# Layer 1's K, Q and V scaled by bounds, wider weight blocks, two maps apart, first weights on another queue

## The chip, the cores and the metric

One core of one Trainium2 chip. The metric is the device time of one execution of the kernel in microseconds (us). The inputs lie in device memory (HBM) in f32 before the execution starts, and the output is written there.

## The reference

A backbone of two layers over 1024 latent and 256 context tokens of width 1024. The normalisation comes after the branch, the modulation `h = x * (1 + scale) + shift` ahead of it. Layer 0 is multi-head latent attention with 16 heads, layer 1 differential attention with 8 heads: each head has two attention maps over the same values.

```python
def combine(o1, o2, gate):
    o = o1 - lam_full.astype(o1.dtype) * o2
    o = rms_norm(o, g_sub) * (1.0 - lambda_init)
    return gated(o, gate)
q, k, v, gate = jnp.split(t @ w_in, 4, axis=-1)
...
s = jnp.einsum('bqhgd,bkhd->bhgqk', qb, k).astype(jnp.float32) * scale
p = jax.nn.softmax(s, axis=-1).astype(v.dtype)
return jnp.einsum('bhgqk,bkhv->bqhgv', p, v)
...
x = layer_norm(DEEPNORM_ALPHA * x + gate[:, None, :] * (o @ out_w[i]), ln_g[i], ln_b[i])
```

In layer 1 q, k and v have 64, 64 and 128 columns per map and head; q and k of the latent tokens get a rotary embedding; the latent queries see all 1280 keys, and the context's own output isn't needed.

## The kernel before, in words

Layer 0 fills the span up to 825 us, its output projection (`out_tile`) goes to 986 us. That projection leaves h of layer 1 as two fp16 parts, `h1H` and `h1L`: for each tile of 128 tokens VectorE (DVE) multiplies the transposed tile by the modulation's scale (L917, into `hb`), GpSimd (POOL) adds the shift (L919), ScalarE (ACT) casts to fp16 (L922), and POOL takes the rest (L923).

Every product of layer 1 is made of three fp16 matmuls (`mm3`, L185 to L187): high by high, high by low, low by high. To make the two parts, `split16` (L181, L182) scales an f32 tile by a power of two and casts it on ACT, and DVE takes the rest. The scale comes from `pow2_of` (L284 to L287), four tiny DVE instructions.

`prod_w(h, which)` loads the weights of a head: `which` 0 is the 256 columns of Q and K, 1 those of V and the gate. Four DMAs of 256 KB from SyncE's queue (SP) bring `ws`; ACT sums the squares (L977, `wsq`); a matmul with ones (L981) adds them over the partitions; DVE and POOL make the scale of it (L983 to L988, `uw`); `split16` makes `wH` and `wL` of each block.

`prod_k1`, `prod_q1` and `prod_v1` make K, Q and V of a head. The rotary embedding leaves K in `kr`; its largest value is taken on DVE (L1064), and `split16` scales by it (`kH`, `kL`; ACT and DVE). Q takes the reciprocal scale. V is evicted from PSUM to `Vf`, the gate to `gg` (L1125, L1126, ACT), both scaled by the weights' scale; DVE takes V's maximum over the row (L1132), a step later the matmul L1141 turns it round, and `split16`'s two halves make `vh` and `vl`.

`scores1` does one tile of 128 queries for both maps. PE computes a PSUM bank of scores of the 256 context keys for the two maps (the first bank), then two banks of 512 keys for each map (L1166, L1167); DVE takes a maximum, negated, of each (L1179, L1183), the smallest of two (L1184), and of these and the context's (L1186, times the softmax scale); ACT takes the exponential of each bank with it (L1189, into `p`), with the sums. Then DVE combines the two maps into one (L1192 to L1195). `turn1` turns the combined map 128 columns at a time (PE, L1202) and splits it (`ph`, `pl`); `values1` multiplies by V (L1210 to L1212).

The order. In layer 1 PE's instructions stand in the order in which the code issues them; those of the other engines are put in order by a scheduler, with a higher priority for scores, turns and values. All engines take their queue in order. `step1` issues one step: scores of tile t, values of tile t-2, then the three turns (4, 4 and 2 blocks) of tile t-1, and after each of the four a slot of side work (`some`), which spends a credit of 3600 matmul columns (`SLOT1`) on a generator that makes the next head's K and Q, then V, with the weights of the sets that follow woven in at the steps of `WAT`. A head has eight steps. A step's maxima of K and V (`later`) are issued at its end. Tiles of PSUM come from eight banks in turn.

Before the first head runs (986 to 1050 us), `prod_w(0, 0)` and `prod_w(0, 1)` are issued in full, then head 0's K, Q and V. During head 6 there is no weight set left, and the output weights of layer 1 (`out_w1`, 512 columns at a time) are loaded in their place; the last head has the output projection beside it, and opens with `out_open`, which converts the other output weights (L1239, L177).

```python
for (k0, n), v in zip(((0, 4), (4, 4), (8, 2)), at[1:]):
    if pc is not None:
        with tc.high_priority(HP):
            turn1(pc, ph, pl, k0, n)
    some(side, v)
```

## Time and profile before

| what | value |
|---|---|
| median of 3 runs | 1907.2 us (1903.72 to 1908.63) |
| the profiled execution | 1901.87 us |
| its span in the trace | 1900.1 us |
| mean granted clock of TensorE | 0.965 of full |
| busy: PE, DVE, ACT, POOL | 1700.0, 1318.6, 1108.2, 853.0 us |

The profile is of one execution. PE is TensorE's matmul stream, PEld its loads of stationary operands, which overlap. A row of a timeline gives an instruction's start, its length, engine, line, operation, output and inputs; in brackets it has how long the engine was idle before it, and what ended that. A row of waits gives who waited for whom: us in total, times, the longest.

### The profile page before, as it was taken

How to read it: one execution, taken by the hardware profiler on the slowest of the kernel's cores; microseconds unless marked ns; L12 is line 12 of the kernel's file. 1: busy time of each engine (PE TensorE's matmuls, PEld its weight loads, DVE VectorE, ACT ScalarE, POOL GpSimd, SP SyncE). 2: the span in 40 equal slices, each digit the busy share in tenths (PEclk: the TensorE clock that was granted, in tenths of full speed). 3: DMA queues.
4: the chain of work that ended last, by engine and by line, in shares of the span. 5: the costliest groups of instructions: out<-in, count | busy, mean ns of one | idle time of the engine just before them, and what ended most of it. 6: DMA issues, size and time to landing. Idle time of an engine off the chain costs nothing. (4 is left out here: it accounts for less than half of the span.)

```text
span 1900.1 us, 37206 instructions
## 1 busy us (share of the span) xinstructions
PE 1700.0 (89%) x14482; PEld 1239.3 (65%) x14482; DVE 1318.6 (69%) x2396; ACT 1108.2 (58%) x2245; POOL 853.0 (45%) x748
## 2 busy tenths in 40 slices
PE   7899979989899899968869999999999999887898
PEld 4888945656566565556656576767676767665776
DVE  7546476595665767626754778787878787987774
ACT  3442157767677678811123677776777676766542
POOL 1441036757667676746652223232232233433544
PEclk9999989999999999979989999999999999999899
DMA  8255531131211212153333111211121212213341
GB/s 297 65 136 151 167 92 40 41 83 24 75 44 32 66 43 76 51 172 132 112 123 98 42 54 47 58 47 48 50 53 42 63 41 64 74 41 132 100 129 67
DMA packets 117663, 155.43 MB, mean 82 GB/s; under 512 B 14591, under 2 KB 85855, under 8 KB 117486
## 3 DMA queue, kind: packets, MB, share of 16 engines
q1 hardware_dynamic: 111726, 147.80, 26.3%
q10 hardware_dynamic: 5760, 5.25, 0.8%
q8 instruction: 114, 1.87, 0.4%
q14 instruction: 63, 0.52, 0.1%
HBM read 99.17 MB, written 27.08 MB: 66 GB/s over the span
## 5 line engine op out<-in xcount | busy, mean ns | idle before, releaser
L709 POOL TENSOR_TENSOR pl<-p,ph 128x1024 f16<-128x1024 f32 (+1 forms) x176 | 367.8, 2095 | 173.6 <-ACT ph L708 154.3
L1189 ACT ACTIVATE p<-ps_b,mx 128x512 f32<-128x512 f32 (+1 forms) x384 | 233.1, 622 | 67.1 <-DVE mx L1186 67.1
L707 ACT ACTIVATE p<-ps_a,esc 128x1024 f32<-128x1024 f32 (+1 forms) x176 | 189.2, 1075 | 123.1 <-PE ps_a L765 116.4
L689 DVE TENSOR_REDUCE mx<-ps_a 128x1 f32<-128x1024 f32 x128 | 155.2, 1221 | 105.1 <-PE ps_a L687 104.9
L708 ACT CAST ph<-p 128x1024 f16<-128x1024 f32 (+1 forms) x176 | 177.2, 1007 | 5.5
L1183 DVE TENSOR_REDUCE mx<-ps_b 128x1 f32<-128x512 f32 x256 | 166.2, 681 | 1.0 <-PE ps_b L1167 0.3
L182 DVE SCALAR_TENSOR_TENSOR pl<-ps_b,lcf,ph 128x512 f16<-128x512 f32 (+1 forms) x192 | 122.7, 655 | 63.4 <-ACT ph L181 63.3
L778 PE MATMUL ps_d<-Vh,pl 128*128 128x65 f16 x1344 | 151.7, 195 | 7.3 <-POOL pl L709 6.0
L775 PE MATMUL ps_d<-Vh,ph 128*128 128x65 f16 x1344 | 154.8, 196 | 0.0
L777 PE MATMUL ps_d<-Vl,ph 128*128 128x64 f16 x1344 | 153.4, 194 | 0.0
L185 PE MATMUL ps_b<-h1H,wH 128*128 128x512 f16 (+1 forms) x384 | 134.0, 349 | 12.5 <-ACT p L1189 12.5
L185 PE MATMUL ps_b<-wH,h1H 128*128 128x256 f16 x512 | 139.5, 272 | 5.6 <-ACT p L1189 5.6
L1166 PE MATMUL ps_b<-KS,QS 128*128 128x512 f16 (+1 forms) x384 | 129.4, 354 | 11.7 <-DVE pl L182 7.7
L775 PEld LDWEIGHTS <-ph 128*128 128x128 f16 x1344 | 125.0, 98 | 22.6 <-issue 5.6
L187 PE MATMUL ps_b<-wH,h1L 128*128 128x256 f16 x512 | 139.5, 273 | 0.0
L186 PE MATMUL ps_b<-wL,h1H 128*128 128x256 f16 x512 | 139.5, 272 | 0.0
L763 PE MATMUL ps_a<-qH,KH 100*128 100x512 f16 x320 | 123.7, 387 | 15.0 <-DVE qH L699 7.5
L181 ACT ACTIVATE ph<-ps_b,lcf 128x512 f16<-128x512 f32 (+1 forms) x192 | 119.4, 636 | 29.8 <-PE ps_b L1202 29.7
L777 PEld LDWEIGHTS <-ph 128*128 128x128 f16 x1344 | 125.6, 99 | 16.1 <-issue 0.6
L186 PE MATMUL ps_b<-h1L,wH 128*128 128x512 f16 (+1 forms) x384 | 134.2, 349 | 0.0
L187 PE MATMUL ps_b<-h1H,wL 128*128 128x512 f16 (+1 forms) x384 | 133.9, 349 | 0.0
L1167 PE MATMUL ps_b<-KS,Q 128*128 128x512 f16 (+1 forms) x384 | 132.4, 353 | 0.0
(380 smaller groups left out, 5202.3 us busy)
## 6 DMA issues: line engine op xcount, KB each, us to landing
adw<-in_ada_w SPq DMA_DIRECT2D x64, 256.0 KB, 2.9
ws<-in_dw SPq DMA_DIRECT2D x64, 256.0 KB, 3.0
g<-sg_d SPq DMA_DIRECT2D x18, 512.0 KB
adaw<-in_ada_w SPq DMA_DIRECT2D x16, 512.0 KB, 5.4
sg_d<-gg ACTq DMA_DIRECT2D x40, 128.0 KB, 2.9
o<-o_d SPq DMA_DIRECT2D x10, 512.0 KB, 9.0
o_d<-op SPq DMA_DIRECT2D x7, 640.0 KB
xt<-in_xT SPq DMA_DIRECT2D x16, 256.0 KB, 2.6
```

The costliest lines, as they stand in the source:

```text
L185: pe.matmul(ps, aH, bH, start=start, stop=False, skip_group_check=skip)
L186: pe.matmul(ps, aH, bL, start=False, stop=False, skip_group_check=skip)
L187: pe.matmul(ps, aL, bH, start=False, stop=stop, skip_group_check=skip)
L689: dve.tensor_reduce(mx[:, t, 0:1], ps, axis=AX.X, op=ALU.max)
L707: act.activation(p32[:, :n], st, AF.Exp, scale=esc0)
L708: act.copy(ph[:, :n], p32[:, :n])
L709: pool.tensor_tensor(pl[:, :n], p32[:, :n], ph[:, :n], op=ALU.subtract)
L775: pe.matmul(pv[:, t, :], ph[:, ts], Vh[:, k, h, :], start=(k == kcs[0] and t == 0), stop=False, skip_group_check=True)
L777: pe.matmul(pv[:, t, :V0], ph[:, ts], Vl[:, k, h, :], start=False, stop=False, skip_group_check=True)
L778: pe.matmul(pv[:, t, :], pl[:, ts], Vh[:, k, h, :], start=False, stop=(k == NT - 1), skip_group_check=True)
L1183: dve.tensor_reduce(mx[:, 2 + 2 * m + i:3 + 2 * m + i], b, axis=AX.X, op=ALU.max, negate=True)
L1189: act.activation(p[m][:, c0:c0 + n], b, AF.Exp, bias=nb, scale=sc1, accum_out=sm[:, 2 + 3 * m + i:3 + 3 * m + i])
```

## The change

- `h1_range`, which runs once before layer 1, makes constant scales: `kc1` for K and V, `hic` and `vic` for the others. The maxima of K (L1064) and of V (L1132), the matmul L1141, and the scales that hung on them are removed. V and the gate are evicted with plain copies; the scale of the gate goes into the Silu. Q is scaled by `es1`, which takes in the softmax scale, so L1184 and L1186 are one instruction, and the exponential has no scale.
- A weight set comes in two DMAs of 512 KB, and its squares and splits are of 1024 columns (half as many); `out_w1` likewise. The tags `ws`, `wL` and `wH` keep their bytes, in half as many buffers (3, 4 and 4 in place of 6, 8 and 8). `WAT` has five places in place of nine.
- `scores1` yields after each map: in `step1`, a side slot stands between the first map's scores and the second's. Five slots of 2900 columns take the place of four of 3600. The last head's order stays.
- `prod_w(0, 0)` is loaded from ACT's queue. `prod_w(0, 1)` is woven into head 0's K and Q instead of being issued ahead of them.

```diff
-WAT = ((6, 10, 14, 18, 23, 28, 32, 36, 39), (3, 7, 11, 15, 20, 25, 29, 33, 36))
+WAT = ((6, 14, 21, 27, 34), (3, 10, 18, 25, 32))
...
-QK1 = 16.0
 PW = 16.0
-SLOT1 = 3600, 3600, 3600, 3600
-SLOTO = 7000, 7000, 7000, 7000
+SLOT1 = 2900, 2900, 2900, 2900, 2900
+SLOTO = 0, 7000, 7000, 7000, 7000
...
         for i in range(2):
             dve.tensor_reduce(hm[:, i:i + 1], ab1[:, i, :, :].rearrange("p a b -> p (a b)"), axis=AX.X, op=ALU.max,
                               apply_absolute_value=True)
-        dve.scalar_tensor_tensor(hm[:, 2:3], hm[:, 0:1], 1.01 * D ** 0.5, hm[:, 1:2], op0=ALU.mult, op1=ALU.add)
-        pe.matmul(bk[:, :P], hm[:, 2:3].to_broadcast([P, P]), idn, start=True, stop=True)
-        dve.tensor_reduce(hm[:, 3:4], bk[:, :P], axis=AX.X, op=ALU.max)
-        dve.tensor_scalar_max(hm[:, 3:4], hm[:, 3:4], 1e-30)
-        pow2_of(hsc, hun, hm[:, 3:4], 16384.0, hm[:, 0:2])
+            pe.matmul(bk[:, i * P:(i + 1) * P], hm[:, i:i + 1].to_broadcast([P, P]), idn, start=True, stop=True)
+        dve.tensor_reduce(hm[:, 2:4], bk[:, :2 * P].rearrange("p (a b) -> p a b", a=2), axis=AX.X, op=ALU.max)
+        R = D ** 0.5
+        dve.tensor_scalar(hm[:, 2:3], hm[:, 2:3], 1.01 * R, 1e-30, op0=ALU.mult, op1=ALU.add)
+        dve.tensor_tensor(hm[:, 4:5], hm[:, 2:3], hm[:, 3:4], op=ALU.add)
+        dve.scalar_tensor_tensor(hm[:, 5:6], hm[:, 3:4], R, hm[:, 2:3], op0=ALU.mult, op1=ALU.add)
+        pow2_of(hsc, hun, hm[:, 4:5], 16384.0, hm[:, 6:8])
+        dve.tensor_tensor(hm[:, 5:6], hm[:, 5:6], hsc, op=ALU.mult)
+        pow2_of(kc1, kci, hm[:, 5:6], 2.0 ** -5, hm[:, 6:8])
+        dve.tensor_scalar_mul(hic, kci, SC1)
...
-    def prod_w(h, which, bank_=lambda: bank("b")):
+    wt, un, us1, es1 = {}, {}, {}, {}
+
+    def prod_w(h, which, bank_=lambda: bank("b"), load=sp):
         wt[which] = []
         ws, sq = [], w1("sq")
-        for q in range(4):
+        for q in range(2):
             ws.append(w1("ws"))
-            sp.dma_start(ws[q], dw[q * 256:(q + 1) * 256, h, which * 256:(which + 1) * 256].rearrange(
+            load.dma_start(ws[q], dw[q * 512:(q + 1) * 512, h, which * 256:(which + 1) * 256].rearrange(
                 "(k p) c -> p k c", p=P))
-            if q % 2:
-                yield 0
-        for q in range(4):
+        yield 0
+        for q in range(2):
             act.activation(w1("wsq"), ws[q].rearrange("p a b -> p (a b)"), AF.Square, accum_out=sq[:, q:q + 1])
-            if q % 2:
-                yield 0
+        yield 0
         bk = bank_()
-        pe.matmul(bk[:, :4], ones, sq, start=True, stop=True)
+        pe.matmul(bk[:, :2], ones, sq, start=True, stop=True)
         u, p2 = w1("uw"), w1("uw")
-        dve.tensor_reduce(u[:, 0:1], bk[:, :4], axis=AX.X, op=ALU.add)
+        dve.tensor_reduce(u[:, 0:1], bk[:, :2], axis=AX.X, op=ALU.add)
         pool.tensor_scalar(u[:, 0:1], u[:, 0:1], 1.01, 1e-30, op0=ALU.mult, op1=ALU.add)
         pool.tensor_tensor(u[:, 0:1], u[:, 0:1], poshalf, op=ALU.pow)
         pow2_of(u[:, 1:2], u[:, 0:1], u[:, 0:1], 16384.0, p2)
-        dve.tensor_scalar(u[:, 0:1], u[:, 0:1], hun, 1.0 if which else QK1 ** 0.5, op0=ALU.mult, op1=ALU.mult)
+        dve.tensor_tensor(u[:, 0:1], u[:, 0:1], hun, op=ALU.mult)
+        if which:
+            us1[h] = w1("us")
+            pool.tensor_tensor(us1[h], u[:, 0:1], vic, op=ALU.mult)
+        else:
+            es1[h] = w1("es")
+            dve.tensor_scalar(es1[h], u[:, 0:1], u[:, 0:1], hic, op0=ALU.mult, op1=ALU.mult)
         un[which] = u[:, 0:1]
         yield 0
-        for q in range(4):
+        for q in range(2):
             wH, wL = w1("wH"), w1("wL")
             split16(wH, wL, ws[q], u[:, 1:2])
-            wt[which] += [(wH[:, j, :], wL[:, j, :]) for j in range(2)]
+            wt[which] += [(wH[:, j, :], wL[:, j, :]) for j in range(4)]
             yield 0
-    for which in range(2):
-        for _ in prod_w(0, which, lambda: bank("c")):
-            pass
+    for _ in prod_w(0, 0, lambda: bank("c"), act):
+        pass
...
+    dve.tensor_tensor(vic, kci, lcf[:, 1:2], op=ALU.mult)
...
         def fin():
-            dve.tensor_reduce(kq[:, 2:3], kr, axis=AX.X, op=ALU.max, apply_absolute_value=True)
-            dve.tensor_scalar_max(kq[:, 2:3], kq[:, 2:3], 1e-30)
-            pow2_of(kq[:, 0:1], kq[:, 1:2], kq[:, 2:3], 256.0, w1("p2s"))
-            dve.tensor_scalar(kq[:, 1:2], kq[:, 1:2], uq, uq, op0=ALU.mult, op1=ALU.mult)
             H, L = w1("kH"), w1("kL")
-            split16(H, L, kr, kq[:, 0:1])
+            split16(H, L, kr, kc1)
...
-            split16(H, L, rr, ksc[h][:, 1:2])
+            split16(H, L, rr, es1[h])
...
-        act.activation(vT, ps[:, :CTX], AF.Copy, scale=uv)
+        act.copy(vT, ps[:, :CTX])
...
+            act.copy(Vf[:, t, :], ps[:, :P])
             if t < 8:
-                act.activation(Vf[:, t, :], ps[:, :P], AF.Copy, scale=uv)
-                act.activation(gg[:, t, :], ps[:, P:256], AF.Copy, scale=uv)
-            else:
-                act.copy(Vf[:, t, :], ps[:, :P])
-        us = w1("us")
+                act.copy(gg[:, t, :], ps[:, P:256])
         def top():
-            dve.tensor_reduce(va[:, 0:1], Vf.rearrange("p t d -> p (t d)"), axis=AX.X, op=ALU.max,
-                              apply_absolute_value=True)
+            split16(vh, vl, Vf, kc1)
             g = gg.rearrange("p t d -> p (t d)")
-            act.activation(g, g, AF.Silu)
+            act.activation(g, g, AF.Silu, scale=uv)
             sp.dma_start(sg_d[1][:SEQ, h * P:(h + 1) * P].rearrange("(t p) d -> p t d", p=P), gg)
-            return fin
-
-        def fin():
-            bk = bank("b")
-            pe.matmul(bk[:, :P], va[:, 0:1].to_broadcast([P, P]), idn, start=True, stop=True)
-            dve.tensor_reduce(va[:, 2:3], bk[:, :P], axis=AX.X, op=ALU.max)
-            dve.tensor_scalar_max(va[:, 2:3], va[:, 2:3], 1e-30)
-            pow2_of(va[:, 1:2], us, va[:, 2:3], 1024.0, w1("p2s"))
-            pool.tensor_tensor(us, us, lcf[:, 1:2], op=ALU.mult)
-            vh = w1("vh")
-            vl = w1("vl")
-            act.activation(vh, Vf, AF.Copy, scale=va[:, 1:2])
-            dve.scalar_tensor_tensor(vl, Vf, va[:, 1:2], vh, op0=ALU.mult, op1=ALU.subtract)
-            vt[h], us1[h] = (vh, vl), us
...
-            dve.tensor_tensor(mx[:, 2 * m + 2:2 * m + 3], mx[:, 2 * m + 2:2 * m + 3], mx[:, 2 * m + 3:2 * m + 4], op=ALU.min)
             nb = mx[:, 6 + m:7 + m]
-            dve.tensor_scalar(nb, mx[:, 2 * m + 2:2 * m + 3], mx[:, m:m + 1], sc1, op0=ALU.min, op1=ALU.mult)
+            dve.tensor_scalar(nb, mx[:, 2 * m + 2:2 * m + 3], mx[:, 2 * m + 3:2 * m + 4], mx[:, m:m + 1],
+                              op0=ALU.min, op1=ALU.min)
             for i, (c0, n, b) in enumerate(((0, 512, st[0, (m,)]), (512, 512, st[512, (m,)]),
                                             (SEQ, CTX, st[SEQ, (0, 1)][:, m * CTX:(m + 1) * CTX]))):
-                act.activation(p[m][:, c0:c0 + n], b, AF.Exp, bias=nb, scale=sc1,
+                act.activation(p[m][:, c0:c0 + n], b, AF.Exp, bias=nb,
                                accum_out=sm[:, 2 + 3 * m + i:3 + 3 * m + i])
-        yield
+            yield
...
-        for hh in range(2):
-            c = slice(hh * 512, hh * 512 + 512)
-            ws = ws_of()
-            sp.dma_start(ws, out_w[1, k * P:(k + 1) * P, c])
-            yield
-            dve.scalar_tensor_tensor(ws, ws, gsub, gate1[:, c], op0=ALU.mult, op1=ALU.mult)
-            split(oHL[k][0][:, c], oHL[k][1][:, c], ws, e_lo=pool)
-            yield
+        ws = ws_of()
+        sp.dma_start(ws, out_w[1, k * P:(k + 1) * P, :])
+        yield
+        dve.scalar_tensor_tensor(ws, ws, gsub, gate1, op0=ALU.mult, op1=ALU.mult)
+        split(oHL[k][0], oHL[k][1], ws, e_lo=pool)
+        yield
...
-        for _ in chain(prod_k1(0), prod_q1(0, 0), prod_q1(0, 1),
+        for _ in chain(weave(chain(prod_k1(0), prod_q1(0, 0), prod_q1(0, 1)), prod_w(0, 1), WAT[0]),
...
         def step1(cur, side, at):
                 if cur:
                     S = scores1(*cur)
                     next(S)
+            some(side, at[0])
+            with tc.high_priority(HP):
+                if cur:
+                    next(S)
                 if turned:
                     values1(*turned.pop(0))
-            some(side, at[0])
+            some(side, at[1])
             pc = None
             if joined:
                 c_, pc, sm = joined.pop(0)
                 ph, pl = w1("ph"), w1("pl")
                 turned.append((*c_, ph, pl, sm))
-            for (k0, n), v in zip(((0, 4), (4, 4), (8, 2)), at[1:]):
+            for (k0, n), v in zip(((0, 4), (4, 4), (8, 2)), at[2:]):
...
-                                WAT[1] if h + 2 < H1 else range(1, 40, 2)))
+                                WAT[1] if h + 2 < H1 else range(1, 40, 4)))
```

What it moves, first on PE, where layer 0's last tile ends and layer 1's first K begins. `z` is the tile turned (`ps_d`), `sq` the sums of squares of a weight set, and `wH`, `h1H` are the parts of K's product. Before:

```order
L187 MATMUL ps_b_12309<-oH_10736,tL_12262 128x512
L915 MATMUL ps_d_12346<-idr,z_12277 128x128 x4
L915 MATMUL ps_d_12353<-idr,z_12277 128x128 x4
L981 MATMUL ps_c_12432<-sq_12395,ones 128x4
L981 MATMUL ps_c_12474<-sq_12457,ones 128x4
L185 LDWEIGHTS wH_12393
L185 MATMUL ps_b_12523<-h1H,wH_12393 128x512
```

After the change:

```order
L187 MATMUL ps_b_12321<-oH_10740,tL_12274 128x512
L921 MATMUL ps_d_12358<-idr,z_12289 128x128 x4
L921 MATMUL ps_d_12365<-idr,z_12289 128x128 x4
L985 MATMUL ps_c_12435<-sq_12406,ones 128x2
L185 LDWEIGHTS wH_12404
L185 MATMUL ps_b_12475<-h1H,wH_12404 128x512
L186 LDWEIGHTS wH_12404
```

One norm matmul (L981, now L985) is left ahead of the first product; the second set's stands later, in the K and Q of head 0.

On DVE, one step in the half of a head that makes K and Q: `mx` are the maxima of a tile, `uw` a weight scale, `kr` the K of the next head. Before:

```order
L1184 TENSOR_TENSOR mx_14580<-mx_14580 128x1
L1183 TENSOR_REDUCE mx_14580<-ps_b_14607 128x1
L983 TENSOR_REDUCE uw_14665<-ps_b_14663 128x1
L1186 TENSOR_SCALAR mx_14580<-mx_14580 128x1
L1057 COPY kr_14342<-ps_b_14548 128x256
L284 TENSOR_SCALAR uw_14666<-uw_14665 128x1
L1184 TENSOR_TENSOR mx_14580<-mx_14580 128x1
L1064 TENSOR_REDUCE kq_14676<-kr_14342 128x1
L285 RECIPROCAL uw_14666<-uw_14666 128x1
L287 TENSOR_SCALAR uw_14665<-uw_14666 128x1
L1186 TENSOR_SCALAR mx_14580<-mx_14580 128x1
```

After the change:

```order
L1164 TENSOR_REDUCE mx_14465<-ps_b_14500 128x1
L1166 TENSOR_SCALAR mx_14465<-mx_14465 128x1
L1164 TENSOR_REDUCE mx_14465<-ps_b_14504 128x1
L182 SCALAR_TENSOR_TENSOR wL_14560<-ws_14277,uw_14449,wH_14559 128x1024
L1166 TENSOR_SCALAR mx_14465<-mx_14465 128x1
L182 SCALAR_TENSOR_TENSOR wL_14614<-ws_14279,uw_14449,wH_14613 128x1024
L182 SCALAR_TENSOR_TENSOR kL_14622<-kr_14184,kc_92,kH_14621 128x1280
```

The maximum over K is gone from between the two minima, which are one instruction (L1166); the wide weight splits stand around them.

On ACT, in the half of a head that makes V, where the weights of the head after the next are split and the next set's squares taken (`wsq`); `o` is a finished tile. Before:

```order
L181 ACTIVATE wH_15580<-ws_15081,uw_15367 128x512
L181 ACTIVATE wH_15617<-ws_15083,uw_15367 128x512
L977 ACTIVATE wsq_15935,sq_15753<-ws_15876 128x512
L1215 ACTIVATE o_2404_15534<-ps_b_15503,sm_15116 128x128
L977 ACTIVATE wsq_15937,sq_15753<-ws_15878 128x512
L1216 ACTIVATE o_2405_15535,ss_15536<-o_2404_15534 128x128
L1189 ACTIVATE p_2396_15469,sm_15468<-ps_b_15477,mx_15467 128x512
```

After the change:

```order
L181 ACTIVATE wH_14094<-ws_13529,uw_13804 128x1024
L1170 ACTIVATE p_2103_13839,sm_13838<-ps_b_13847,mx_13837 128x512
L1170 ACTIVATE p_2103_13839,sm_13838<-ps_b_13851,mx_13837 128x512
L1170 ACTIVATE p_2103_13839,sm_13838<-ps_b_13841,mx_13837 128x256
L1170 ACTIVATE p_2104_13840,sm_13838<-ps_b_13874,mx_13837 128x512
L1170 ACTIVATE p_2104_13840,sm_13838<-ps_b_13878,mx_13837 128x512
L1170 ACTIVATE p_2104_13840,sm_13838<-ps_b_13841,mx_13837 128x256
L181 ACTIVATE ph_13933<-ps_b_13935,lcf 128x512
L1125 COPY Vf_13459<-ps_b_13861 128x128
L1127 COPY gg_13458<-ps_b_13861 128x128
L1125 COPY Vf_13459<-ps_b_13950 128x128
L181 ACTIVATE ph_13933<-ps_b_13964,lcf 128x512
```

The squares stood right behind the split whose buffer their load takes over; now the exponentials (L1189, now L1170) of both maps and some evictions stand between, and the squares come two rows further on.

## Rows read from the trace of the kernel before

**Rows 1.** Windows by stage; the first line names the columns.

```profile
core 0: us, PE busy (x) PEld busy (x) DVE busy (x) ACT busy (x) POOL busy (x), PEclk, DMA share, GB/s
1066.00:1640.00 574.00, 531.88 (x4517) 389.73 (x4516) 470.91 (x1062) 417.27 (x1156) 169.92 (x266) 0.99 0.19 53
1640.00:1725.70 85.70, 77.70 (x670) 57.94 (x668) 71.15 (x155) 55.72 (x157) 33.69 (x42) 0.98 0.14 38
1725.70:1767.00 41.30, 23.97 (x166) 15.88 (x166) 36.46 (x58) 24.70 (x60) 25.16 (x25) 0.81 0.51 166
1051.60:1054.60 3.00, 3.00 (x8) 1.06 (x7) 2.77 (x8) 0.65 (x1) 0.19 (x1) 0.50 0.58 175
```

**Rows 2.** PE's waits, 1066 to 1640 us, six heads: us, times, longest.

```profile
PE ps_b L185 <- ACT p L1189: 16.9, 12, 1.9
PE ps_b L1202 <- DVE mx L1184: 7.3, 6, 1.4
PE ps_b L1166 <- DVE pl L182: 6.6, 6, 1.1
PE ps_b L1210 <- ACT gg L1126: 4.9, 6, 0.9
PE ps_b L1202 <- DVE pl L182: 3.5, 6, 0.6
```

**Rows 3.** PE's timeline, one head, 1180 to 1245 us, rows with a gap.

```profile
1182.32 0.38 PE L1166 MATMUL ps_b<-KS,QS 128*128 128x512 f16 x1 [1.11 <-DVE pl L182]
...
1192.90 0.27 PE L185 MATMUL ps_b<-h1H,wH 128*128 128x256 f16 x1 [1.89 <-ACT p L1189]
...
1201.40 0.63 PE L1202 MATMUL ps_b<-idr,p 128*128 128x128 f32 x4 [1.43 <-DVE mx L1184]
...
1237.41 0.27 PE L185 MATMUL ps_b<-wH,h1H 128*128 128x256 f16 x1 [1.07 <-ACT p L1189]
```

**Rows 4.** DVE's timeline around the maximum over K.

```profile
1175.05 1.48 DVE L1064 TENSOR_REDUCE kq<-kr 128x1 f32<-128x1280 f32 x1
...
1176.56 0.20 DVE L1186 TENSOR_SCALAR mx<-mx 128x1 f32<-128x1 f32 x1
```

**Rows 5.** DVE's timeline, a step later.

```profile
1190.44 0.15 DVE L1184 TENSOR_TENSOR mx<-mx 128x1 f32<-128x1 f32 x1
...
1191.83 0.21 DVE L1186 TENSOR_SCALAR mx<-mx 128x1 f32<-128x1 f32 x1
```

**Rows 6.** ACT's timeline in the V half of that head.

```profile
1234.65 0.63 ACT L977 ACTIVATE wsq<-ws 128x512 f32<-128x512 f32 x1 [2.63 <-DMA ws<-in_dw]
```

**Rows 7.** Timelines of PE, POOL and ACT at the start of layer 1.

```profile
998.29 0.58 PE L981 MATMUL ps_c<-sq,ones 128*128 128x4 f32 x2 [11.91 <-ACT wsq L977]
998.74 0.59 PE L185 MATMUL ps_b<-h1H,wH 128*128 128x512 f16 x1
...
987.72 2.04 POOL L919 TENSOR_TENSOR hb<-hb,ab 128x512 f32<-128x512 f32 x2
...
991.28 2.56 ACT L181 ACTIVATE wH<-ws,uw 128x512 f16<-128x512 f32 x4 [0.44 <-DVE uw L286]
```

**Rows 8.** PE's timeline ahead of head 0 and of the last head.

```profile
1050.51 0.49 PE L1141 MATMUL ps_b<-idr,va 128*128 128x128 f32 x2 [1.98 <-DVE va L1132]
...
1730.01 0.49 PE L1141 MATMUL ps_b<-idr,va 128*128 128x128 f32 x2 [4.28 <-DVE va L1132]
```

**Rows 9.** Groups by line and shape, whole span: busy us, mean ns.

```profile
L182 DVE SCALAR_TENSOR_TENSOR wL<-ws,uw,wH 128x512 f16<-128x512 f32 x64 | 50.1, 795 | 1.3 <-ACT wH L181 1.3
L182 DVE SCALAR_TENSOR_TENSOR stkL<-ps_a,ksc,stkH 128x1024 f16<-128x1024 f32 x8 | 10.3, 1284 | 1.1 <-ACT stkH L181 0.3
L181 ACT ACTIVATE stkH<-ps_a,ksc 128x1024 f16<-128x1024 f32 x8 | 8.9, 1107 | 0.0
```

**Rows 10.** PE's timeline of side work, two matmuls on end.

```profile
1184.42 0.38 PE L185 MATMUL ps_b<-h1H,wH 128*128 128x512 f16 x1
1184.64 0.38 PE L186 MATMUL ps_b<-h1L,wH 128*128 128x512 f16 x1
```

38 lines of the change are left out of this document (14 added, 24 removed).

## The prediction

> **What bounds the kernel now.** I read the views from wide to narrow. The table of windows by stage comes first [rows 1]: over the six heads between 1066 and 1640 us PE is busy for 531.88 of 574.00 us at a clock of 0.99, DVE for 470.91 and ACT for 417.27. PE sets the pace there, and only what makes PE wait is worth anything. In the turn to the last head, 1725.7 to 1767 us, PE works for 23.97 of 41.30 us, and DVE for 36.46.
>
> The table of PE's waits over the same six heads says what the 42 idle us are [rows 2]: five lines, each of them once or twice per head, 39.2 us together or 6.5 us a head. Every releaser is an instruction of DVE or ACT. The timeline of one head shows the same thing as single gaps [rows 3]: four of its six stand there (the other two belong to the last two lines of rows 2, some 0.6 and 0.8 us a head), three of them in the half in which K and Q of the next head are made, one in the half that makes V. A head has eight steps, one for each tile of 128 queries, and takes some 96 us (574/6), so most steps have no gap.
>
> Why those engines are late, from their own timelines. DVE is full between 1175 and 1202 us. Between the minimum of a tile, L1184, and L1186, whose result the exponentials wait for, it does the maximum over K, L1064, 1.48 us [rows 4]. A step later a weight split and a Q split stand between the same two lines, which start 1.39 us apart [rows 5]. The exponentials start late, so p, its turning, and the PSUM banks that they read are late. In the V half ACT stands 2.63 us at L977, the square of a weight block whose DMA has not landed, with exponentials queued behind it in order [rows 6].
>
> At the start of layer 1 [rows 7] PE waits 11.91 us for L981, the norm of the *second* weight set, which the written order puts ahead of all of head 0, although the first set's wH splits began at 991.28. That first set waits for POOL, which adds the shift to the last tile's hb until 989.76 before it gets to the norm.
>
> At both turns between stages V stops PE [rows 8]: 1.98 us at 1050.51 and 4.28 us at 1730.01, for the maximum over V (1.48 us on DVE) that the matmul L1141 turns round.
>
> **The change, part by part.** *First weights by ScalarE, second set woven in.* PE's order loses L981 of the second set. The new first matmul waits for the first wH, now 1024 wide: 991.28 plus 1.107 us (the nearest row, a 128x1024 split of layer 0 [rows 9]) is 992.4 instead of 998.74, a gain of 6.3. The third matmul needs wL, another 1.284 us [rows 9], while PE has two matmuls of some 0.4 us each: a stall of about 0.45. Net **-5.9**. ScalarE issues the loads behind its cast of a tile, later than SP did; POOL, which gets to the norm only after 989.76, covers that. Should the cover fail I take 2 us less; with no stall and a little less on POOL it is 7. Bounds -4 to -7.
>
> The Trainium skill, "DMA: Bandwidth & Descriptors", section Issuing engines are not separate DMA queues, says that issuing on another engine saves only the sequencer's time, since all transfers share the same 16 engines. By that the new queue is worth nothing here and the gain is all from PE's order; the 11.91 us wait for the second set's squares [rows 7] agrees, and I have given the queue no term.
>
> *K, Q, V by bounds.* The bounds cost a few tiny instructions and a second 128-column matmul before layer 1, where PE idles for other reasons: nothing, and were that cover gone, under 1 us. Per head DVE loses L1064 (1.48), L1132 (1.48) and a dozen tiny instructions. V's split no longer waits for the turned maximum. Copies replace scaled evictions of the same size on ACT, which is not full [rows 1]: nothing.
>
> *Boundary before head 0.* The 1.98 us go, and with them the matmuls behind them that run at a granted clock of 0.50 [rows 1], the 1.2 GHz level: seven, and such a one takes 0.59 instead of 0.38 us [rows 7, 10], another 1.5. The V copies, the Silu and a table load stay ahead of the first exponentials, so I take **-2.5**, between 0 and -3.5.
>
> *Six heads.* In the K/Q half the maximum over K is gone and L1184 and L1186 become one instruction, so nothing can stand between them; in the two steps concerned the exponentials start 1.3 to 1.5 us earlier. The gaps there (1.11, 0.58, 1.89 and 1.43 in the head shown) end on that chain, 5.0 us; I take 3.0, since the wide wL and kL splits still share DVE with the combine. In the V half the square that waited for its DMA now stands a dozen ACT instructions behind the split that frees its buffer, with a whole tile's exponentials between: I take 1.2 of the two gaps (1.07, 0.92). 4.2 a head, six heads: **-25**. Bounds: 1.0 a head, -6 (only the shortest chain gets better), and all of it, -39.
>
> *Wide blocks.* Four splits of 795 ns become two of about 1284 [rows 9]: DVE gives back 0.6 us a set. But each piece holds its queue 0.49 us longer. Both lie in the numbers above; alone I cost it at nothing, covered by the gap of a tile's step, and bound it below as a rival. Weight loads of 512 KB in place of 256: DMA is 0.19 busy in the heads [rows 1], nothing.
>
> *Two maps apart.* PE does 2900 columns of side work between the first map's scores and the second's. A matmul of 512 columns starts 0.22 us after the one before [rows 10], so the second map is 1.2 us later; the first map's exponentials can run meanwhile. The five slots hold 14,500 columns instead of 14,400, so the rest of the step shrinks little. Part of the 4.2.
>
> *Head 6* has the same side work, with output weights in the V half: PE idles for 8.0 us of its 85.70 [rows 1], as much as in the others, but the extra output weights are in longer pieces now. **-3**, between +1 (two of them 0.49 us late) and -8.0.
>
> *Turn to the last head.* The 4.28 us go. If the eight matmuls behind are as slow as those at the other boundary, 0.21 each is another 1.7. But DVE is the full engine there with L1239, and conversions of 1024 columns now block it longer: **-4**, between 0 and -6.
>
> Sum: -5.9 - 2.5 - 25 - 3 - 4 = -40.4. It is made against the profiled execution, 1901.87 us, which lies 5.3 us (0.28%) under the median of the three runs, 1907.2. Such a spread, about 0.3%, is what a measurement of this kernel can tell from nothing. On the median's basis: **1867 us**.
>
> **Rivals.** *Only the ends gain.* DVE is 82% busy in the heads, and after the K maximum the wide splits are next in its queue: the same gaps come back under other names. For it: the gap at 1182.32 waits for pl, a split, and not for the maximum itself. Against: the gaps are 0.6 to 1.9 us each, no more than the 1.48 us that leave DVE's queue ahead of them. Then -5.9 - 2.5 - 4 and a little: -15, 1892.
>
> *Wide pieces hold up the queues.* Each of four pieces a head is 0.49 us longer on DVE and no more than that on ACT; if each one's length lands on the exponentials or their maxima, 0.49 x 4 x 2 x 7 is 27 us, and 1894 is left. It needs a piece in front of a critical instruction every time; the order has them behind the maxima in the step I looked at. The Trainium skill, "Perfetto Trace Analysis", section Optimizing Scalar/DVE Operations, gives the rule: where Scalar or Vector are not saturated but cause bubbles on other engines, break instructions up. It speaks against this part of the change; the trace bears it out in the splits ahead of L1186 [rows 5], but the merged instruction takes away the place where such a piece stood, so I give it the small chance.
>
> *Slower: the second map is late in every step.* Its exponentials, the combine and the turning all shift by 1.2 us. If PE then waits so much in each of the 56 steps, +67 stands against -40: 1934, +27. It decides at 40.4/56 = 0.72 us a step. For: the join already ends a gap of 1.43 us once per head, at 1201.40. Against: it does so in one step of eight, so the others have slack, and ACT, 73% busy, can do the first map's exponentials meanwhile.
>
> *All head gaps go.* -39 and -8.0 in place of -25 and -3: -59, 1848.
>
> *It does nothing*, because PE waits for whatever DVE does last: about 1905.
>
> **How the numbers follow.** Forecast (1852 to 1882) 0.58; only the ends 0.14; wide pieces 0.08; all gaps 0.08; second map late 0.07; nothing 0.05. The first four are faster: 0.88; same 0.05; slower 0.07. The range leaves out the slower case, the case of nothing and the far end of the wide pieces: 1846 to 1897.
>
> **What would show it.** First layer-1 matmul at about 992.4, no PE wait for a norm before it. No V wait at the two turns. PE's waits in six heads: about 14 us instead of 39, with no L1184-type minimum among the releasers. A head's period of some 92 us instead of 96. It is wrong if PE waits for p, pl or a turn in most steps (second map late), or if wL or wH stand before the waited-for DVE and ACT instructions (wide pieces).

## The result and the profile after

The changed kernel takes 1875.4 us, median of 4 runs (1874.68 to 1881.57), beside 1905.46 us for the kernel before on the same chip (4 runs): a ratio of 0.9848, with a 95% interval of 0.9821 to 0.9875, or 30 us less. 1867 us was forecast, from 1846 to 1897. The sign and the range were right, and three quarters of the gain came. But it did not come from where the sum had put most of it.

The windows by stage of the changed kernel, cut at its own head starts: heads 0 to 5, head 6, the turn to the last head (columns as in [rows 1]).

```profile
1043.90:1609.36 565.46, 530.27 (x4481) 385.47 (x4480) 435.04 (x869) 392.92 (x1078) 151.83 (x261) 1.00 0.20 53
1609.36:1708.73 99.37, 90.07 (x758) 65.77 (x756) 79.23 (x143) 64.92 (x181) 36.88 (x49) 0.97 0.16 44
1708.73:1747.00 38.27, 25.15 (x190) 18.77 (x188) 33.31 (x50) 27.35 (x66) 21.62 (x19) 0.87 0.53 182
```

[rows 1] cuts its six heads 15 us behind their start. Cut at its own head starts, the kernel before has in heads 0 to 5

```profile
1050.83:1625.93 575.10, 533.59 (x4491) 388.63 (x4488) 469.73 (x1064) 411.80 (x1142) 167.78 (x263) 0.99 0.18 51
```

So six heads are 9.7 us shorter, and DVE does 35 us less in them. PE idles for 35.2 us in place of 41.5. It is also busy for 3.3 us less, and that fits the clock: before, three stretches of 3.4 us in these heads had a granted clock of 0.50 (one of them is in [rows 1]), now one; 6.8 us less at half the clock make 3.4 us. PE's waits over the same six heads:

```profile
PE ps_b L1183 <- ACT p L1170: 14.9, 17, 2.6
PE ps_b L185 <- DVE pl L182: 6.0, 5, 1.2
PE ps_b L185 <- ACT p L1170: 4.3, 13, 0.4
PE ps_b L1123 <- ACT p L1170: 3.8, 6, 0.6
PE ps_b L1147 <- ACT o L1196: 2.8, 6, 1.0
PE ps_b L1147 <- DVE pl L182: 2.7, 5, 0.8
```

34.5 us, where [rows 2] had 39.2. The minima that [rows 2] names are gone from the releasers, as they should be, and others stand in their place.

Where the gain came from is best read between PE's own marks: the start of the last transposes of layer 0 (z, line 915, now 921), of the first matmul of layer 1, of each head's first score, and PE's last matmul. Layer 0 is the same code in every kernel here, yet its last transposes began anywhere from 983.8 to 992.2 us into the span. So stages, counted from z, tell variants apart that the medians can't. In us:

| kernel | z to first matmul | to head 0 | head 0 | heads 1-5 | head 6 | last head on | sum from z | median |
|---|---|---|---|---|---|---|---|---|
| before | 14.5 | 52.1 | 93.1 | 482.0 | 104.4 | 160.5 | 906.6 | 1905.5 |
| changed | 8.3 | 50.5 | 89.1 | 476.3 | 99.4 | 156.5 | 880.1 | 1875.4 |
| blocks of 512 | 7.8 | 50.9 | 88.2 | 476.1 | 98.5 | 159.6 | 881.2 | 1878.4 |
| maps together | 8.3 | 50.6 | 91.5 | 474.8 | 102.2 | 160.0 | 887.3 | 1883.0 |
| old start | 15.8 | 49.5 | 89.0 | 476.7 | 99.3 | 156.7 | 886.9 | 1882.7 |
| bounds alone | 15.3 | 49.6 | 89.9 | 478.2 | 97.6 | 162.0 | 892.6 | 1891.0 |
| four ws buffers | 8.3 | 50.4 | 89.0 | 478.1 | 97.2 | 157.0 | 879.9 | 1878.0 |
| first loads by SP | 8.3 | 50.7 | 89.0 | 475.8 | 99.7 | 156.7 | 880.2 | 1877.5 |
| Q low on POOL | 8.3 | 54.7 | 87.1 | 468.4 | 97.6 | 156.8 | 873.0 | 1869.5 |
| norms early | 8.3 | 50.5 | 87.1 | 481.3 | 97.4 | 155.8 | 880.4 | 1880.7 |
| both | 8.3 | 52.3 | 90.9 | 495.1 | 95.4 | 155.8 | 897.7 | 1896.7 |
| Q low on POOL, mended | 8.3 | 50.7 | 86.1 | 461.1 | 96.4 | 156.8 | 859.4 | 1856.3 |

The stages of a row are those of one execution. In heads 1 to 5 PE has the same instructions in the same order in "changed", "old start", "first loads by SP" and "four ws buffers", and these take 475.8 to 478.1 us, so differences of up to some 2 us in that column say little. The medians come from several chips, on which the kernel before took 1905.5 to 1908.4 us. The runs with the weights' low parts on POOL and with the values in the third turn's bank are not in the table; their heads are 6 and 38 us longer.

Five full heads gained 5.7 us in all, 1.1 each; PE's idle time in them fell from 34.5 to 30.6 us. The other 20.8 us of the 26.5 lie around them.

One head of the changed kernel, PE's timeline, the rows with a gap; they answer to [rows 3]:

```profile
1349.37 0.39 PE L185 MATMUL ps_b<-h1H,wH 128*128 128x512 f16 x1 [1.24 <-DVE pl L182]
...
1356.12 0.65 PE L1183 MATMUL ps_b<-idr,p 128*128 128x128 f32 x4 [0.37 <-ACT p L1170]
...
1360.81 0.38 PE L1147 MATMUL ps_b<-KS,QS 128*128 128x512 f16 x1 [0.35 <-ACT o L1196]
...
1371.37 0.44 PE L1183 MATMUL ps_b<-idr,p 128*128 128x128 f32 x2 [2.03 <-ACT p L1170]
...
1387.04 0.38 PE L1147 MATMUL ps_b<-KS,QS 128*128 128x512 f16 x1 [0.48 <-DVE pl L182]
...
1393.26 0.27 PE L185 MATMUL ps_b<-wH,h1H 128*128 128x256 f16 x1 [0.35 <-ACT p L1170]
...
1403.97 0.33 PE L1123 MATMUL ps_b<-idr,rr 128*128 128x128 f32 x1 [0.64 <-ACT p L1170]
1404.63 0.27 PE L185 MATMUL ps_b<-wH,h1H 128*128 128x256 f16 x1 [0.33 <-ACT p L1170]
...
1405.76 0.66 PE L1183 MATMUL ps_b<-idr,p 128*128 128x128 f32 x4 [0.31 <-ACT p L1170]
```

The largest, 2.03 us, waits for a PSUM bank that exponentials have not yet read. Why they were late stands in the timelines of DVE and ACT ahead of it:

```profile
1362.47 1.54 DVE L1176 SCALAR_TENSOR_TENSOR p<-p,sm,p 128x1280 f32<-128x1280 f32 x1
1366.58 0.75 DVE L182 SCALAR_TENSOR_TENSOR kL<-rr,es,kH 128x512 f16<-128x512 f32 x1 [2.56 <-ACT kH L181]
1367.25 0.68 DVE L1160 TENSOR_REDUCE mx<-ps_b 128x2 f32<-128x512 f32 x1
1367.85 2.47 DVE L1164 TENSOR_REDUCE mx<-ps_b 128x1 f32<-128x512 f32 x4
```

```profile
1364.78 1.06 ACT L982 ACTIVATE wsq<-ws 128x1024 f32<-128x1024 f32 x1 [2.70 <-DMA ws<-in_dw]
...
1365.84 0.71 ACT L181 ACTIVATE kH<-rr,es 128x512 f16<-128x512 f32 x1
...
1370.54 0.69 ACT L1170 ACTIVATE p<-ps_b,mx 128x512 f32<-128x512 f32 x1 [2.74 <-DVE mx L1166]
```

The squares of a weight block, a whole 1024 columns now, wait 2.70 us on ACT for their DMA; Q's high part (`kH`) stands behind them, Q's low part (`kL`) on DVE waits for that, and five maxima of a tile whose scores PE had finished by 1363.6 wait behind it until 1367.25. What is new there is the place of `kL`. The square and `kH` behind it were late before, too (rows of the kernel before):

```profile
1185.24 0.63 ACT L977 ACTIVATE wsq<-ws 128x512 f32<-128x512 f32 x1 [1.90 <-DMA ws<-in_dw]
...
1187.83 0.72 ACT L181 ACTIVATE kH<-rr,kq 128x512 f16<-128x512 f32 x1 [1.18 <-POOL rr L1044]
```

But `kL` then stood behind that tile's maxima, between its last minimum and L1186 (the Q split of [rows 5]), and did not wait.

In the V half the square stands later, as the prediction read from the order, and waits for 0.49 us in place of 2.63. But ACT now stands there 3.84 us at a weight split, whose scale is late, ahead of exponentials:

```profile
1401.06 2.19 ACT L181 ACTIVATE wH<-ws,uw 128x1024 f16<-128x1024 f32 x2 [3.84 <-DVE uw L286]
```

On the mean of heads 1 to 5 the gaps of the K/Q half fell from 4.9 to 4.0 us, and those of the V half went from 2.0 to 2.1.

The start went as worked out: the first matmul at 993.39, its wL 0.79 us late.

```profile
993.39 0.61 PE L185 MATMUL ps_b<-h1H,wH 128*128 128x512 f16 x1 [6.09 <-ACT wH L181]
...
995.21 0.61 PE L187 MATMUL ps_b<-h1H,wL 128*128 128x512 f16 x1 [0.79 <-DVE wL L182]
```

### The profile page after: what moved, and what is told of

It is laid out like the page before. It is cut to its first block, busy times and chain, and to the rows that moved or that the text cites. A ratio compares the mean times of both kernels' runs of the same rounds, so it can differ in the third digit from the quotient of the medians.

```text
span 1874.0 us, 36684 instructions
## 1 busy us (share of the span) xinstructions
PE 1693.5 (90%) x14468; PEld 1236.2 (66%) x14468; DVE 1272.7 (68%) x2132; ACT 1076.1 (57%) x2141; POOL 830.0 (44%) x740
## 5 line engine op out<-in xcount | busy, mean ns | idle before, releaser
L1170 ACT ACTIVATE p<-ps_b,mx 128x512 f32<-128x512 f32 (+1 forms) x384 | 230.3, 617 | 73.8 <-DVE mx L1166 73.5
L769 PE MATMUL ps_a<-qH,KH 100*128 100x512 f16 x320 | 123.4, 386 | 15.8 <-DVE qH L705 8.1
L1147 PE MATMUL ps_b<-KS,QS 128*128 128x512 f16 (+1 forms) x384 | 125.3, 344 | 9.3 <-DVE pl L182 5.5
L784 PEld LDWEIGHTS <-pl 128*128 128x128 f16 x1344 | 124.4, 98 | 11.0 <-POOL pl L715 10.9
L1148 PE MATMUL ps_b<-KS,Q 128*128 128x512 f16 (+1 forms) x384 | 128.6, 344 | 0.0
L1195 POOL TENSOR_TENSOR sm<-sm,us 128x1 f32<-128x1 f32 x64 | 17.7, 276 | 249.1 <-DVE sm L1174 245.1
```

Of the source, the lines that this page charges most:

```text
L784: pe.matmul(pv[:, t, :], pl[:, ts], Vh[:, k, h, :], start=False, stop=(k == NT - 1), skip_group_check=True)
L1170: act.activation(p[m][:, c0:c0 + n], b, AF.Exp, bias=nb, accum_out=sm[:, 2 + 3 * m + i:3 + 3 * m + i])
```

## The experiments

Theory Q began from the rival with the wide pieces: blocks of 1024 in the in-order queues took back the heads' gain. Theory M put it on the second map's lateness, theory W on the reverse of Q. The first three runs undo one part each, and the fourth leaves only the bounds.

**Blocks of 512.** Loads, squares, splits, `out_w1` and `WAT` as before.

```diff
-    TAGP = {"ws": ([P, 4, 256], F32, 3), "wL": ([P, 4, 256], F16, 4), "wH": ([P, 4, 256], F16, 4),
+    TAGP = {"ws": ([P, 2, 256], F32, 6), "wL": ([P, 2, 256], F16, 8), "wH": ([P, 2, 256], F16, 8),
```

> The changed kernel with weight blocks (and output-weight pieces) of 512 columns as before; bounds, two maps apart and the new start stay. Theory Q (queues): the heads gained only 1.1 us each because wide squares and splits now stand in ACT's and DVE's order ahead of exponentials and maxima; with narrow pieces a head should take about 92 to 93.5 us instead of 95 and the kernel about 1860 to 1868 us. Theory M (maps): the second map's lateness ate the gain; blocks don't matter, 1873 to 1878 us. Theory W (the wide blocks are themselves what gains, by fewer instructions on a full DVE): slower, 1880 to 1888 us.

1878.41 us, 0.9865 (0.9844 to 0.9887), an interval that overlaps the changed kernel's. Heads 1 to 5 take 476.1 us, as with wide blocks, with gaps of 6.1 us a head in other places (in the second full head 0.30, 1.86, 1.28, 1.16 and 1.42 in five steps). From z it is 1.1 us slower: 0.9 faster in head 0 and in head 6 each, and 3.1 slower in the last stage, where PE stands 9.76 us for one `tL` (7.33 in the changed kernel). Theory Q in this form falls, and theory W with it: the width decides nothing in the full heads. The Trainium skill, "Perfetto Trace Analysis", section Optimizing Scalar/DVE Operations, says that breaking instructions up may allow work to be done sooner where ScalarE and VectorE are not saturated but cause bubbles on other engines. It brought nothing in these heads: 476.1 us with blocks of 512, 476.3 with 1024.

**Maps together.**

```diff
-SLOT1 = 2900, 2900, 2900, 2900, 2900
+SLOT1 = 0, 3600, 3600, 3600, 3600
```

> The changed kernel with the two maps' scores on end again (no side slot between them, four slots of 3600). Theory M: the second map's lateness ate the gain, so this is faster, 1862 to 1870 us. Theory Q: the slot between the maps matters little or helps by a little, since exponentials of the first map start before the second's scores: 1873 to 1882 us.

1882.95 us, 0.9888 (0.9866 to 0.9910). From z 7.2 us slower; but the five full heads are 1.5 us faster, which is within what equal heads differ by. Beside wide blocks the slot is worth 2.4 us in head 0, 2.8 in head 6 and 3.5 in the last stage, and nothing in the middle. Theory M falls.

**Old start.**

```diff
-    for _ in prod_w(0, 0, lambda: bank("c"), act):
+    for _ in prod_w(0, 0, lambda: bank("c")):
...
+    for _ in prod_w(0, 1):
+        pass
...
-        for _ in chain(weave(chain(prod_k1(0), prod_q1(0, 0), prod_q1(0, 1)), prod_w(0, 1), WAT[0]),
+        for _ in chain(prod_k1(0), prod_q1(0, 0), prod_q1(0, 1),
```

> The changed kernel with the first two weight sets loaded by SP and the second set's norm ahead of head 0's K again. Both theories of the heads: only the start differs, the first matmul of layer 1 comes 5 to 6 us later and 1 to 2 us are given back in head 0's production, so 1879 to 1882 us.

1882.65 us, 0.9881 (0.9853 to 0.9909): from z 6.9 us more, 7.5 at the start and 1.0 back in the production.

**Bounds alone**: the three edits above together.

> The kernel before with the bounds alone (K, Q, V scales; merged minimum): blocks of 512, maps together, old start. Theory Q: most of the gain lies in the bounds, and the narrow blocks keep it in the heads: a head 92 to 94 us, total 1872 to 1882 us. Theory M says the same or a little better. If the bounds alone give only the two turns between stages (V's maximum), heads stay at 96 us and the total is 1893 to 1898 us.

1891.04 us, 0.9925 (0.9897 to 0.9952). From z 14.0 us less than before, and of that only 3.8 in heads 1 to 5, although 4.1 us a head left DVE (79.2 us in a head before, 75.1 here). The four parts sum to 29 us from z (14.0, 6.9, 7.2, 1.1) against 26.5 measured. Stage by stage they do not add up: head 6 is shorter with the bounds alone (97.6) than with all four parts (99.4), and the last stage is longer than before (162.0 against 160.5).

All these kernels, whatever waits they had, took 95 to 96 us a head. Three theories remained. S: the wait for the squares' DMA is what holds the changed kernel's head. B: eight PSUM banks conserve the waits. L: they follow DVE's load. The next three runs were to try them, and a fourth the queue of the first weights.

**Four ws buffers.**

```diff
-"o2": ([P, P], F32, 2)
+"o2": ([P, P], F32, 1)
...
-"ws": ([P, 4, 256], F32, 3)
+"ws": ([P, 4, 256], F32, 4)
...
-"wsq": ([P, D], F32, 1)
+"wsq": ([P, D], F16, 1)
```

> The changed kernel with four buffers of ws in place of three (room made by an fp16 scratch for the squares and one buffer less of another scratch), so that a weight block's load waits for no split and its square no longer stands on ACT for 2.7 us with exponentials behind. Theory S (that wait costs what it seems to cost): the wait of 2.0 us in each head's fourth step goes, heads take 93 us, 1862 to 1868 us. Theory B (the waits are conserved: with eight PSUM banks PE runs close behind the exponentials' release of them, and one late piece replaces another): the wait goes from ACT, heads still take 94.5 to 95.5 us, 1872 to 1878 us.

1878.04 us, 0.9854 (0.9818 to 0.9889). The squares wait 0.63 us instead of 2.70, and the gap stays at 1.96: theory S falls. The timelines of ACT and DVE at the same place say why:

```profile
1368.18 0.72 ACT L181 ACTIVATE kH<-rr,es 128x512 f16<-128x512 f32 x1 [1.90 <-POOL rr L1054]
```

```profile
1368.94 0.75 DVE L182 SCALAR_TENSOR_TENSOR kL<-rr,es,kH 128x512 f16<-128x512 f32 x1 [2.50 <-ACT kH L181]
1369.61 0.68 DVE L1160 TENSOR_REDUCE mx<-ps_b 128x2 f32<-128x512 f32 x1
```

Behind the squares there was a second cause, just as late: POOL's last step of the rotary embedding (in the changed kernel it starts at 1364.46 and takes 1.27 us, so it ends 0.1 us ahead of the squares). What both go through is one instruction, `kL` of Q, which stands on DVE ahead of the maxima.

**The weights' low parts on POOL.**

```diff
-            split16(wH, wL, ws[q], u[:, 1:2])
+            act.activation(wH, ws[q], AF.Copy, scale=u[:, 1:2])
+            pool.tensor_scalar(ws[q], ws[q], u[:, 1:2], None, op0=ALU.mult)
+            pool.tensor_tensor(wL, ws[q], wH, op=ALU.subtract)
```

> The changed kernel with the low parts of the weights made by GpSimd (two passes) and not by DVE: some 5 us a head leave DVE. Theory L (the waits follow DVE's load): heads 92 to 93.5 us, 1858 to 1868 us. Theory B: a small gain, since exponentials wait for maxima a little less, heads 94 to 95 us, 1868 to 1875 us; slower if POOL's passes make DVE slower while they run.

1934.3 us, 1.0157 (1.0117 to 1.0197), slower than before, heads of 101 to 104 us. POOL holds `ws` longer (its two passes over a block take 2.85 and 2.13 us), so the next load comes late, and the squares wait on ACT with everything behind them (ACT's waits from 1045 to 1610 us, five heads and a half):

```profile
ACT wsq L982 <- DMA ws<-in_dw: 75.8, 24, 7.0
```

It says nothing on theory L, for it added a wait with the load that it took. It shows what such a wait costs. Theory L is answered by the runs above: in heads 1 to 5 the bounds alone take 20.5 us off DVE (396.0 to 375.5) and 3.1 us off PE's idle time, and narrow blocks give DVE 8.0 us more than wide ones (373.7 and 365.8) while the heads take as long (476.1 and 476.3).

**Values in the third turn's bank.**

```diff
-                    values1(*turned.pop(0))
...
+                        st = turn1(pc, ph, pl, k0, n)
+                        if vals and k0 == 8:
+                            values1(*vals, st[:, 2 * P:3 * P])
```

> The changed kernel with the values of a tile issued behind the third turn, into the free half of that turn's PSUM bank: eight banks claimed in a step instead of nine, plus the side work's. Theory B: each bank has some 1 us more until it is claimed again, the waits for exponentials and splits shrink by half or more, heads 91.5 to 93.5 us, 1855 to 1868 us. Theories S and L: nothing on the named waits, 1872 to 1880 us.

2119.5 us, 1.1114 (1.1074 to 1.1155). The values then wait for the split of the blocks that they share the bank with (PE's waits from 1045 to 1610 us, some four heads):

```profile
PE ps_b L1192 <- DVE pl L182: 123.9, 33, 6.0
```

So it tested another thing than the number of banks, and theory B was left to the runs below.

**First loads by SP.**

```diff
-    for _ in prod_w(0, 0, lambda: bank("c"), act):
+    for _ in prod_w(0, 0, lambda: bank("c")):
```

> The changed kernel with its first weights issued by SP again, the second set still woven in. Prediction: the queue is worth nothing, POOL's late norm sets the start: first matmul within 0.5 us of 993.4, 1874 to 1878 us. If the queue matters: 2 us or more later.

1877.5 us, 0.985 (0.9817 to 0.9884). The first matmul comes 8.25 us after z, as in the changed kernel: the queue is worth nothing, as predicted. (By the span it came at 998.29, outside of what was expected; layer 0 ended 4.9 us later in that run.)

Theory D says that each wait is the price of one instruction that stands in an in-order queue ahead of its time. The decisive run takes that instruction away.

**Q's low part on POOL.** PE's order in heads 1 to 5 stays; on DVE both `kL` of Q go. At the place in question the order around it stays; elsewhere some rows change places.

```diff
-            split16(H, L, rr, es1[h])
+            act.activation(H, rr, AF.Copy, scale=es1[h])
+            pool.tensor_scalar(rr, rr, es1[h], None, op0=ALU.mult)
+            pool.tensor_tensor(L, rr, H, op=ALU.subtract)
```

> The changed kernel with the low part of Q made by GpSimd in two passes, not by DVE; every other row of DVE's order stays. In the changed kernel Q's low part stands in DVE's order ahead of a tile's maxima and waits there 2.5 us for ScalarE and GpSimd, in each head's fourth step. Theory D (a wait is the price of one instruction that stands in an in-order queue ahead of its time): that step's gap of 2.3 us goes and the others stay, heads 92.6 to 93.2 us instead of 95, from the last transpose to the end of PE 868 to 872 us instead of 880, total 1863 to 1869 us. Theory B (eight PSUM banks conserve the waits, whoever causes them): heads 94.5 to 95.5 us, total 1873 to 1878 us.

1869.49 us, 0.9819 (0.9791 to 0.9847). DVE's timeline at that place:

```profile
1362.19 1.53 DVE L1178 SCALAR_TENSOR_TENSOR p<-p,sm,p 128x1280 f32<-128x1280 f32 x1
1363.65 0.67 DVE L1162 TENSOR_REDUCE mx<-ps_b 128x2 f32<-128x512 f32 x1
```

The maxima follow the combination at once. The step's gaps fall from 2.3 to 0.35 us in heads 2 to 5 and a head from 95.3 to 93.7 us. Theory B is wrong there: the gap went, and with it most of its time. Theory L fails as well: DVE has 3.0 us less to do in five heads, and PE idles 6.9 us less. But theory B had half a point: a new wait of 1.2 us a head came in the next step (PE for the turn, behind ACT's copy of V's context into `rr`, which POOL still reads), and head 0's production lost 4.2 us.

```profile
1378.22 0.66 PE L1185 MATMUL ps_b<-idr,p 128*128 128x128 f32 x4 [1.17 <-ACT rr L1115]
```

**Norms early**, alone and with the edit above.

```diff
-WAT = ((6, 14, 21, 27, 34), (3, 10, 18, 25, 32))
+WAT = ((6, 14, 16, 27, 34), (3, 10, 12, 25, 32))
```

> The changed kernel with the norm of each weight set some five places earlier in PE's order. Its tiny instructions then leave DVE before a tile's maxima, and ScalarE need not wait at the weight split ahead of the exponentials (3.8 us a head in the V half). Theory D: the V half's gaps of 2.1 us a head shrink to about 1, and in the K/Q half the splits of the turned tile now stand ahead of the combination: 1 to 2 us a head, 1863 to 1871 us. Theory B: other gaps take their place, 1872 to 1878 us.

> Both together, Q's low part on GpSimd and the norms early. Theory D: the two gains add, heads 91 to 92.5 us, 1855 to 1864 us. Theory B: 1870 to 1878 us.

Alone: 1880.68 us, 0.988 (0.9848 to 0.9912), outside of both expectations. The V half gets what was expected, gaps of 0.4 us instead of 2.1. But `kL` of Q now stands ahead of the combination, and the turn waits for that (PE's and DVE's timelines):

```profile
1366.19 1.11 PE L1183 MATMUL ps_b<-idr,p 128*128 128x128 f32 x4 [4.56 <-DVE p L1176]
```

```profile
1363.92 0.75 DVE L182 SCALAR_TENSOR_TENSOR kL<-rr,es,kH 128x512 f16<-128x512 f32 x1 [2.79 <-ACT kH L181]
1364.59 1.55 DVE L1176 SCALAR_TENSOR_TENSOR p<-p,sm,p 128x1280 f32<-128x1280 f32 x1
```

That wait alone does not make the heads longer: in heads 1 to 5 PE idles for 29.3 us, 1.3 less than in the changed kernel. They are 5.0 us longer all the same, because PE is busy for 6.3 us more. Each of the five heads has one such wait, of 4.2 to 5.9 us, and with each the granted clock falls to 0.50 for 3.4 or 6.8 us, 23.9 us in all (3.4 in the changed kernel). PE's row behind the wait shown:

```profile
1366.30:1369.30 3.00, 3.00 (x12) 2.13 (x13) 2.65 (x6) 1.84 (x4) 1.14 (x2) 0.50 0.48 109
```

With both: 1896.73 us, 0.995 (0.9931 to 0.9969), heads of 99 us. The gains did not add, and the expectation was wrong. Against Q's low part on POOL alone, five heads have 16.5 us more of PE's idle time, and PE is busy for 10.2 us more (27.3 us at a clock of 0.50, none without the early norms). The scheduler had put a square ahead of the exponentials in the V half, whose DMA was late:

```profile
1421.63 1.06 ACT L982 ACTIVATE wsq<-ws 128x1024 f32<-128x1024 f32 x1 [5.95 <-DMA ws<-in_dw]
```

**Q's low part on POOL, mended**: head 0 keeps DVE's split, and V's context takes `rsw` in place of `rr`.

```diff
+            if h == 0:
+                split16(H, L, rr, es1[h])
+            else:
...
-        vT = w1("rr")[:, :CTX]
+        vT = w1("rsw")[:, :CTX]
```

> Q's low part on GpSimd from head 1 on (head 0's stays on DVE), and the transposed context V takes the scratch of the rotary embedding, so that it does not wait for GpSimd's second pass. With the low part on GpSimd alone, head 0's production lost 4.2 us and a new wait for that scratch took 1.2 us a head. Theory D (each wait belongs to one instruction ahead of its time): both go, the gap of the fourth step stays away, heads 92 to 92.6 us, 860 to 866 us from the last transpose to PE's end, total 1857 to 1864 us. Theory B: other waits fill in, 1868 to 1873 us.

1856.34 us, median of 5 runs (1852.75 to 1858.90); 0.9721 (0.9701 to 0.9741) of before, clear of the changed kernel's interval. That is a little under what theory D expected (1857 to 1864). Heads 1 to 5 take 461.1 us, 92.2 each; the production is back at 50.7. PE's waits over six heads:

```profile
PE ps_b L185 <- DVE pl L182: 6.0, 5, 1.2
PE ps_b L185 <- ACT p L1175: 4.1, 12, 0.4
PE ps_b L1188 <- ACT p L1175: 3.4, 10, 0.4
PE ps_b L1128 <- ACT p L1175: 3.0, 6, 0.8
PE ps_b L1152 <- ACT o L1201: 2.8, 6, 1.0
PE ps_b L1152 <- DVE pl L182: 0.3, 1, 0.3
```

19.6 us are left of 34.5, and the first line, `pl` behind a combination, was touched by none of these edits. This kernel beats both the kernel before and the changed one.

## Why the prediction was right, and where not

- **The start: right.** 14.5 to 8.3 us from z, 6.3 as worked out, less a stall of 0.79 (0.45 was taken): -5.5 against -5.9. The queue's term of nothing was right.
- **Boundary before head 0: under-sized.** -2.5 was taken, -3.5 as the bound. Production gained 1.6, or 2.4 without the stall counted above, and head 0 2.8 more than a full head: -5.2. Both pieces of the term, V's wait and the slow matmuls, came in full: V's 1.98 us are gone, and in head 0 PE is busy for 1.6 us less, as the stretch at a clock of 0.50 [rows 1] is gone. The rest is head 0's waits, 7.0 to 4.6 us, which the sum had not costed there. The bounds alone give 2.5 of it in the production and most of head 0's; the slot between the maps is worth 2.4 in head 0 where the blocks are wide.
- **Six heads: the step that failed.** -25 was forecast, 4.2 of 6.5 us a head; 1.1 a head came in heads 1 to 5, which makes some -6.8, and only 0.8 a head of that is waiting that went. In the K/Q half 0.9 us of waits went where 3.0 were taken; in the V half none where 1.2 were. The sum treated each gap of [rows 3] as belonging to what stood ahead of it on DVE or ACT, and took the rest of both queues as it was. What left was right: no L1184-type minimum releases PE, and the V half's square waits for 0.49 us. But the orders of DVE and ACT are made by the scheduler, and they were made anew. In the new one another instruction with an unfinished input (`kL` of Q) stands ahead of five maxima, and in the V half a weight split whose scale is late stands ahead of exponentials. The first is shown by the runs without `kL`, the second by the norms made earlier, which took the V half's gaps from 2.1 to 0.4 us. The prediction did look at the new order, at the step with the K maximum, and not at the one after it, where `kL` of Q waits for a `kH` behind a square. The first rival, by which the same gaps come back under other names, describes the heads best; it missed the total (1892) since the ends gave 20 us where the sum had 15, and the heads still 7.
- **Wide pieces: wrong as a mechanism.** With blocks of 512 the heads are the same. It isn't the length of a piece, 0.49 us more, that costs, but its wait for an input. In the last stage the wide pieces even gain 3.1 us.
- **Second map late: not seen.** This rival of the prediction has the wrong sign in the main. In full heads the slot costs 0.3 us each; at the ends, beside wide blocks, it gains 8.7.
- **Head 6: -0.7 for -3**, inside its bounds. The table's column has -5.0, but V's wait of 4.28 us ended at 1730.01, ahead of the last head's first score at 1730.34, and so lies in this column; it belongs to the next term. Without it PE idles for 9.5 us before and 9.3 after. The largest gap that is left has the heads' cause: at 1660.03 PE waits 4.72 us for a combination that stands behind `kL` of Q, which waited for 3.62 us.
- **Turn to the last head: -8.8 for -4, beyond its bound of -6.** 4.28 us are V's wait, and 4.5 come from there to the end of the span. Those are not waiting: from the last head's first score PE idles for 13.1 us in both kernels, and is busy for 4.1 us less. Before, the granted clock was 0.50 for 17.1 us of this stage, now for 10.2. The term had 1.7 us for that.

```profile
1730.34:1891.22 160.88, 147.83 (x936) 114.93 (x933) 107.20 (x214) 77.45 (x194) 83.83 (x82) 0.95 0.38 122
```

```profile
1708.73:1865.59 156.86, 143.74 (x936) 113.66 (x933) 104.48 (x191) 79.58 (x195) 80.77 (x79) 0.97 0.37 126
```

What is late next is what the prediction named: DVE's conversions of the output weights and a combination stand ahead of `tL`, and PE waits once for 7.33 us.

```profile
1730.15 0.50 PE L185 MATMUL ps_b<-oH,tH 128*128 128x512 f32 x1 [1.45 <-ACT tH L176]
...
1738.22 0.80 PE L187 MATMUL ps_b<-oH,tL 128*128 128x512 f32 x1 [7.33 <-DVE tL L177]
```

These sum to -27.0; layer 0 was 0.9 us longer, and the spans differ by 26.1 (1900.1 and 1874.0). The medians say 30: before, the profiled execution lay under its median, after it did not. Of the signs that the prediction named, two came true: V's waits and the L1184-type minima are gone. Two did not: PE's waits in six heads are 34.5 us where it had about 14, and a head takes 95.3 where it had 92. The total was nearer than its terms by luck: the ends were sized too low and the heads too high.

## What to carry to other kernels

In these heads a wait on an in-order engine was the price of one instruction whose input was not there, not of the engine's load: 35 us less on DVE took 6.3 us off PE's waits in six heads, and two instructions of 0.75 us a head, moved to another engine (with one scratch buffer changed for it), gave 15 us in five. Before a gap is booked as gained, read in the new order, row by row through a whole period, what stands ahead of the waited-for instruction and what that waits for itself; then look one cause further, since a second was hidden right behind the first. And compare variants stage by stage from a mark behind the code that they share, with PE's idle and busy time apart: here PE's busy time moved by 3 to 10 us in whole stages, with the time at a clock of 0.50.
